# In-projection of a hybrid trunk: the gates' chunks first, then scan steps and token tiles in turn

## The chip, the core and the metric

The kernel runs on one core of a Trainium2 chip. The metric is the device time in microseconds, the median of several executions. The engines are named as in the profile: PE (TensorE, with PEld for its weight loads), DVE (VectorE), ACT (ScalarE), POOL (GpSimd) and SP (the queue that issues the DMAs). All arithmetic is float32; products are formed from a high and a low part in the fp32r form, three matmuls for each product (`mm3`).

## The reference

Two layers run over 9 tiles of 128 tokens: one tile of context and eight of a latent grid, 1024 features each. A layer multiplies its modulated input by `w_in` and cuts the result into parts:

```python
z = jnp.einsum('bsd,dn->bsn', h, P['w_in'][l])
hq, hff, hfb, hi, hg, mq, mkv, mkr, gq, gk, gv = jnp.split(z, IN_OFFSETS, axis=-1)
```

- hq, hff, hfb, hi and hg feed a gated linear scan (HGRN2), forward and backward, with 4 heads of 64: the two gates are sigmoids of hff and hfb, whose logarithms are summed along the tokens; the scan's query is silu(hq), its value hi; hg gates the scan's output.
- gq, gk and gv are query, key and value of a grouped attention (6 heads, 2 key heads), with an RMS norm of each head and a rotary embedding in two dimensions.
- mq, mkv and mkr feed a latent attention (6 heads).

What scan and attentions give is multiplied by `w_out`, added, normalised, and followed by a SwiGLU mixer. The modulation (`w_ada`) scales and shifts both halves of a layer.

## The kernel before

A layer has phases: `phase_b` (in-projection, scan), `phase_c` (attention), `phase_d` (out-projection), `phase_e` (mixer). The change lies in `phase_b` and `hgrn`.

**Chunks.** `w_in` is stored as eight chunks of 256 columns and one, "b", of 288. Chunk 0 is hq (the scan's query), 1 and 2 are the forward and backward gates, 4 is hi (the scan's value), 3 is hg, 5 is the first half of gq, 6 the rest of gq with gk, "b" is mkv, gv and mkr, 7 is mq. `w_in()` loads a chunk's weights and splits them into a high part (ACT, L103) and a low part (DVE or, for one chunk number, POOL, L104); they lie in a ring of 8 tiles, of which a chunk takes 4 (b: 6).

**Token chunks.** `token_chunk` takes one chunk through the 9 token tiles: 24 matmuls (8 row blocks, three products each, L110 to L112) into one bank, then an evacuation that depends on the chunk. Chunks 1 and 2: two sigmoids on ACT (L379, L380). Chunks 4 and 3: a copy on ACT (L373) and a store. Chunks 5 and 6: square and copy on ACT, a row sum on DVE (L412), an inverse root on POOL (L118, L119), two or three multiplies on DVE (L415, L417), the rotary embedding on POOL (L397 to L401), a store. Chunk b: a smaller form of that (L442 to L452). Chunk 7: L432 to L435. After every other token tile `self.fill()` puts in a half-step of the next modulation (L176), in layer 0 only, 16 half-steps in all. Chunk 0 is computed the other way round: its weights are the stationary operand, and each of six passes streams 384 tokens (L466 stores them by scan tile).

**Gates and scan.** `gates` takes the logarithms, in 9 steps, of both gates (L564 to L570: two Ln on ACT, four operations on DVE each); an ordering edge puts the Ln behind the last sigmoid of chunk 2. `hgrn` then walks over the 9 tiles. For each, `prep` forms the cumulative sums on PE and copies them (L598), loads value and query (L616, L618); `levels` runs 8 levels, -1 to 6: from level 0 on three subtractions on DVE (L641, L644), an Exp on ACT, two products on POOL (L648 for X, L650 for Q), four small matmuls on PE (L655) and two predicated copies on DVE (L660); `out` does the tile's output (L682) and the state's update. `prep` of the next tile is written between levels 2 and 3. X, Q and E have two buffers each.

**What sets the order.** The program is written as one stream. A planner gives each engine its own order: by its own estimate of times it takes, among the instructions whose inputs and buffers are free, the one written first. On the chip each engine follows that order and waits where an input is late. In the text the order is: chunk 0, chunk 1, constants, chunk 2, gates, chunk 4, the whole scan, chunks 3, 5, 6, b, 7 (with the GQA turns, L526 to L542, in chunk 7's evacuation), the gate of the scan's output (`hgrn_gate`, L720 to L729). Accumulators: layer 0 has two banks for chunks, layer 1 three.

Of the kernel before, what the change touches and what calls it, by code (L numbers as in the profile page):

```python
# [16 lines left out]
P = 128  # L17
# [16 lines left out]
TX = 3  # L34

# [18 lines left out]
class Build:  # L54
# [272 lines left out]
    def w_in(self, l, c):  # L327
# [4 lines left out]
        return [(k0, k0 + 4) + self.wsplit(A["w_in_a"][l, c, :, k0:k0 + 4, :], [4, 256], self.nc.gpsimd if c == 0 else None)  # L332
                for k0 in (0, 4)]

    def phase_b(self, l, first=None):
# [18 lines left out]

        def token_chunk(name, evac):
            ws = self.w_in(*name)
            n = 288 if name[1] == "b" else 256
            for t in range(NT):
                ps = self.ps("A")
                terms = [(self.hts(t, k, 0), self.hts(t, k, 1), hi[:, k - k0, :], lo[:, k - k0, :])  # L360
                         for k0, k1, hi, lo in ws for k in range(k0, k1)]
                self.mm3(ps[:, :n], terms)
                evac(t, ps)
                if t % 2:
                    self.fill()

        def stage():
            return self.t("b2", [P, 384], tag="st", bufs=3)
# [85 lines left out]

        ws = first or self.w_in(l, 0)
        for ci in range(3):
            for j in range(2):
                ps = self.ps("A")
                terms = [(hi[:, k - k0, j * P:(j + 1) * P], lo[:, k - k0, j * P:(j + 1) * P],
                          self.HT[ci][:, k, 0, :], self.HT[ci][:, k, 1, :])  # L460
                         for k0, k1, hi, lo in ws for k in range(k0, k1)]
                self.mm3(ps[:, :384], terms)
                sg = stage()
                nc.scalar.activation(sg[:, :384], ps[:, :384], AF.Sigmoid)
                nc.vector.scalar_tensor_tensor(sg[:, :384], ps[:, :384], 64 ** -0.5, sg[:, :384], op0=ALU.mult, op1=ALU.mult)
                nc.sync.dma_start(z["h"][3 * ci:3 * ci + 3, :, j, :].rearrange("t p s -> p t s"),  # L466
                                  sg[:, :384].rearrange("p (t s) -> p t s", t=3))

        token_chunk((l, 1), ev_f(0))
# [959 lines left out]
```

## Time and profile before

| | |
|---|---|
| median of 3 runs | 3788.2 us (3786.13 to 3790.14) |
| the profiled execution | 3788.79 us, span 3787.0 us |
| PE busy | 3667.2 us (97%) |
| DVE busy | 2021.7 us (53%) |
| ACT busy | 1380.3 us (36%) |
| POOL busy | 1100.7 us (29%) |
| mean granted PE clock | 0.981 |

The busy time of PE is a sum over the whole span, and a matmul counts as busy while it waits in PE's pipeline. The granted clock says in which part of a stretch PE ran at the upper of its two levels (1.00 is 2.4 GHz, 0.50 is 1.2 GHz). `phase_b` of layer 0 lies between about 36 and 490 us of the span, that of layer 1 between about 1955 and 2345 us.

### The profile page before, as it was taken

What the parts mean: (1) busy time and instruction counts of PE and PEld (TensorE: products, weight loads), DVE (VectorE), ACT (ScalarE), POOL (GpSimd) and SP (SyncE); (2) the same over time, 40 slices, a digit from 0 to 9 for tenths busy, and PEclk for the clock granted to TensorE, in tenths of its full rate; (3) what the DMA queues carried; (4) which work ended last, traced back from release to release, by engine and by line L of the source; (5) the groups of instructions that cost most, each with busy time, mean ns of one, the idle gap of its engine ahead of it and who ended that gap; (6) DMA issues with size and microseconds to landing.
All of it is one profiled execution on the core that took longest, in us unless ns stands there. A gap on an engine that the chain in (4) does not pass through costs nothing.

```text
span 3787.0 us, 60397 instructions
## 1 busy us (share of the span) xinstructions
PE 3667.2 (97%) x23734; PEld 3210.9 (85%) x23734; DVE 2021.7 (53%) x3906; ACT 1380.3 (36%) x3283; POOL 1100.7 (29%) x1394
## 2 busy tenths in 40 slices
PE   8999899999999999999999989999999999999997
PEld 6878777788788888999989878778877999999996
DVE  3489456556564333333366894665567533333336
ACT  3433466666341111111144335666654211111111
POOL 1158850211161000000432786511126600000054
PEclk9998899999999999999999998999999999999998
DMA  6521421001134331111231115100012311111131
GB/s 240 179 64 43 117 65 25 15 7 35 59 130 157 101 106 51 51 40 48 96 128 59 51 44 140 28 20 15 7 55 73 114 41 47 41 40 45 45 95 73
DMA packets 185967, 263.78 MB, mean 70 GB/s; under 512 B 68657, under 2 KB 114353, under 8 KB 185170
## 3 DMA queue, kind: packets, MB, share of 16 engines
q1 hardware_dynamic: 185682, 259.92, 21.7%
q8 instruction: 187, 3.06, 0.3%
q14 instruction: 98, 0.80, 0.1%
HBM read 218.47 MB, written 38.77 MB: 68 GB/s over the span
## 4 chain that ended last, share of the span: by engine, by line
PE 81%; DVE 7%; POOL 4%; ACT 3%; issue 2%; DMA 2%; SPq 0%; POOLq 0%; DVEq 0%; ACTq 0%
PE b L110 10%; PE b L112 10%; PE b L111 10%; PE d L855 7%; PE c L806 5%; PE a L110 5%; PE b L784 5%; PE a L111 4%; PE a L112 4%; PE a L784 3%; PE b L655 2%; PE c L110 2%; PE c L112 2%; PE c L111 2%; PE d L111 2%
## 5 line engine op out<-in xcount | busy, mean ns | idle before, releaser
L111 PE MATMUL b<-h,w 128*128 128x384 f32 x1848 | 622.4, 337 | 3.6 <-DVE h L104 2.7
L110 PE MATMUL b<-h,w 128*128 128x384 f32 x1848 | 623.8, 338 | 0.1
L112 PE MATMUL b<-h,w 128*128 128x384 f32 x1848 | 621.8, 337 | 0.0
L103 ACT CAST w<-raw 128x1024 fp32r<-128x1024 f32 (+2 forms) x192 | 198.7, 1036 | 803.4 <-PE c L111 262.7
L104 DVE TENSOR_TENSOR w<-raw,w 128x1024 fp32r<-128x1024 f32 (+3 forms) x188 | 242.1, 1295 | 367.9 <-ACT w L103 362.4
L110 PEld LDWEIGHTS b<-h,w 128*128 128x128 f32 x1848 | 347.4, 188 | 17.8 <-issue 7.6
L111 PEld LDWEIGHTS b<-h,w 128*128 128x128 f32 x1848 | 347.6, 188 | 10.3 <-DVE h L104 4.5
L112 PEld LDWEIGHTS b<-h,w 128*128 128x128 f32 x1848 | 347.5, 188 | 8.0 <-issue 5.0
L1245 POOL TENSOR_TENSOR acc<-acc,lg 128x512 f32<-128x512 f32 x36 | 49.1, 1378 | 935.4 <-DVE acc L1231 931.7
L110 PE MATMUL a<-w,h 128*128 128x256 f32 (+1 forms) x960 | 287.2, 299 | 8.4 <-DVE st L445 4.9
L855 PE MATMUL d<-pt,v 128*64 128x128 f32 x3456 | 288.9, 285 | 0.4 <-DVE m L856 0.4
L111 PE MATMUL a<-w,h 128*128 128x256 f32 (+1 forms) x960 | 281.0, 293 | 0.0
L112 PE MATMUL a<-w,h 128*128 128x256 f32 (+1 forms) x960 | 279.7, 292 | 0.0
L806 PE MATMUL c<-ident,p 128*128 128x128 f32 x1728 | 272.0, 279 | 6.7 <-ACT p L790 2.9
L855 PEld LDWEIGHTS d<-pt,v 128*64 128x64 f32 x3456 | 186.3, 136 | 76.7 <-issue 61.7
L785 DVE TENSOR_REDUCE m<-b 128x1 f32<-128x384 f32 x346 | 188.5, 554 | 112.8 <-PE b L784 112.1
L806 PEld LDWEIGHTS c<-ident,p 128*128 128x128 f32 x1728 | 200.4, 141 | 47.2 <-issue 16.3
L790 ACT ACTIVATE p<-b,nm 128x384 f32<-128x384 f32 x346 | 198.6, 582 | 72.4 <-DVE nm L788 66.3
L110 PEld LDWEIGHTS a<-w,h 128*128 128x128 f32 x960 | 188.1, 196 | 30.9 <-ACT m L380 6.7
L111 PEld LDWEIGHTS a<-w,h 128*128 128x128 f32 x960 | 188.1, 196 | 5.4 <-issue 1.9
L112 PEld LDWEIGHTS a<-w,h 128*128 128x128 f32 x960 | 187.5, 195 | 4.2 <-issue 1.7
L1202 DVE TENSOR_TENSOR gate<-gate,b 128x384 f32<-128x384 f32 x110 | 60.9, 553 | 242.5 <-PE b L112 242.5
(391 smaller groups left out, 8483.1 us busy)
## 6 DMA issues: line engine op xcount, KB each, us to landing
w<-in_w_ada_dram SPq DMA_DIRECT2D x96, 512.0 KB, 4.4
raw<-in_w_ffn_in_dram SPq DMA_DIRECT2D x88, 512.0 KB, 3.5
raw<-in_w_ffn_out_dram SPq DMA_DIRECT2D x44, 512.0 KB, 3.6
raw<-in_w_in_a_dram SPq DMA_DIRECT2D x32, 512.0 KB, 4.4
xs<-acc SPq DMA_DIRECT2D x36, 256.0 KB, 4.1
u<-xs SPq DMA_DIRECT2D x36, 256.0 KB, 2.5
raw<-in_w_out_dram SPq DMA_DIRECT2D x16, 512.0 KB, 4.3
tx<-zq SPq DMA_DIRECT2D x72, 96.0 KB, 2.4
```

The lines of the kernel that those rows point to most:

```text
L103: self.nc.scalar.copy(hi, src)
L104: (eng or self.nc.vector).tensor_tensor(lo, src, hi.bitcast(F32), op=ALU.subtract)
L110: self.nc.tensor.matmul(out, ah, bh, start=i == 0, stop=False)
L111: self.nc.tensor.matmul(out, ah, bl, start=False, stop=False)
L112: self.nc.tensor.matmul(out, al, bh, start=False, stop=i == n - 1)
L655: nc.tensor.matmul(ps[:, j * P:(j + 1) * P], X[r, j, :], Q[r, j, :], start=True, stop=True)
L784: nc.tensor.matmul(ps, a, bfn(c * 384, 384), start=k == 0, stop=k == len(ops) - 1)
L785: nc.vector.reduce_max(mx[:, c:c + 1], ps, axis=AX.X)
L790: nc.scalar.activation(pt[:, c * 384:(c + 1) * 384], tiles[c], AF.Exp, bias=nm, accum_out=sm[:, u, c:c + 1])
L806: nc.tensor.transpose(pt[:, (2 * i + u) * P:(2 * i + u + 1) * P], g["p"][u][:, kt * P:(kt + 1) * P], self.ident)
L855: nc.tensor.matmul(po[h * 64:(h + 1) * 64, :P], g["v"](k, h), turned[s // 2][:, o:o + P], start=k == 0, stop=k == 8)
L1202: nc.vector.tensor_tensor(g, g, ps[:, :384], op=ALU.mult)
```

## The change

Three things change in `phase_b`, one in `hgrn`.

- The order of the first chunks becomes 1, 2, gates, 0; the chunk whose low part POOL splits becomes number 1.
- `token_chunk` becomes a generator, `tiles`, that yields after every token tile, runs through several chunks, and asks for the next chunk's weights at token tile 4 of the present one.
- Chunks 4, 3, 5, 6 and b are one such generator. `hgrn` becomes a generator too, which yields after every level and after `out`, nine times for each scan tile; in five of the nine places a token tile is written. Chunk b so moves ahead of the end of the scan's pool; chunk 7 stays where it was.
- The load of the scan's value moves from `prep` to the head of `out`.

```diff
+TILE_TURNS = (0, 2, 4, 6, 7)
...
-        return [(k0, k0 + 4) + self.wsplit(A["w_in_a"][l, c, :, k0:k0 + 4, :], [4, 256], self.nc.gpsimd if c == 0 else None)
+        return [(k0, k0 + 4) + self.wsplit(A["w_in_a"][l, c, :, k0:k0 + 4, :], [4, 256], self.nc.gpsimd if c == 1 else None)
...
+        def tiles(*chunks, ws=None):
+
+            ws = ws or self.w_in(l, chunks[0][0])
+            for i, (name, evac) in enumerate(chunks):
+                n = 288 if name == "b" else 256
+                for t in range(NT):
+                    ps = self.ps("A")
+                    terms = [(self.hts(t, k, 0), self.hts(t, k, 1), hi[:, k - k0, :], lo[:, k - k0, :])
+                             for k0, k1, hi, lo in ws for k in range(k0, k1)]
+                    self.mm3(ps[:, :n], terms)
+                    evac(t, ps)
+                    if t % 2:
+                        self.fill()
+                    if t == 4 and i + 1 < len(chunks):
+                        nxt = self.w_in(l, chunks[i + 1][0])
+                    if t == NT - 1 and i + 1 < len(chunks):
+                        ws = nxt
+                    yield
+
         def token_chunk(name, evac):
...
+            for _ in tiles((name[1], evac)):
+                pass
...
-        ws = first or self.w_in(l, 0)
-        for ci in range(3):
...
-        token_chunk((l, 1), ev_f(0))
+        for _ in tiles((1, ev_f(0)), ws=first):
+            pass
...
         token_chunk((l, 2), ev_f(1))
         self.gates(l)
-        token_chunk((l, 4), ev_raw("i"))
-
-        self.hgrn(l, cst, masks)
-
-        token_chunk((l, 3), ev_raw("g"))
-        token_chunk((l, 5), ev_q(0))
-        token_chunk((l, 6), ev_q(1))
+
+        ws = self.w_in(l, 0)
+        for ci in range(3):
...
+        proj = tiles((4, ev_raw("i")), (3, ev_raw("g")), (5, ev_q(0)), (6, ev_q(1)), ("b", ev_k))
+        for n, _ in enumerate(self.hgrn(l, cst, masks)):
+            if n % 9 in TILE_TURNS:
+                next(proj)
+        for _ in proj:
+            pass
...
-        token_chunk((l, "b"), ev_k)
         token_chunk((l, 7), ev_mq)
...
-            it = self.t("b2", [P, 256], tag="it", bufs=2)
-            nc.sync.dma_start(it, z["i"][t])
...
         def out(t, ops):
...
+            bc, kT, q, at = ops
+            it = self.t("b2", [P, 256], tag="it", bufs=2)
+            nc.sync.dma_start(it, z["i"][t])
...
-            levels(t, ops, -1, 3)
+            yield from levels(t, ops, -1, 3)
             nxt = block(t + 1) if t + 1 < NT else None
-            levels(t, ops, 3, 7)
+            yield from levels(t, ops, 3, 7)
             out(t, ops)
+            yield
             ops = nxt
...
-        first = self.w_in(0, 0)
+        first = self.w_in(0, 1)
```

## Rows read from the trace of the kernel before

**Rows 1.** windows: start:end, length, busy us (x count) of PE, PEld, DVE, ACT, POOL, PEclk, DMA, GB/s

```profile
179.00:240.00 61.00, 61.00 (x431) 47.73 (x429) 46.25 (x110) 23.80 (x49) 27.50 (x33) 1.00 0.26 80
240.00:412.00 172.00, 158.31 (x1109) 138.68 (x1108) 156.92 (x360) 67.40 (x151) 146.65 (x193) 0.90 0.16 48
412.00:490.00 78.00, 65.58 (x463) 62.95 (x463) 17.80 (x40) 30.68 (x90) 49.97 (x109) 0.89 0.51 139
2060.00:2150.00 90.00, 89.18 (x695) 78.46 (x694) 76.65 (x179) 37.89 (x85) 62.11 (x81) 1.00 0.15 44
2150.00:2305.00 155.00, 142.34 (x965) 125.44 (x966) 126.75 (x303) 60.08 (x140) 131.83 (x200) 0.89 0.18 56
2305.00:2345.00 40.00, 35.38 (x286) 33.89 (x284) 12.18 (x22) 22.58 (x62) 32.48 (x58) 0.97 0.74 200
2345.00:2360.00 15.00, 11.03 (x58) 8.95 (x59) 8.14 (x21) 7.45 (x24) 3.21 (x5) 0.63 0.39 105
```

**Rows 2.** waits of TensorE from 240 to 412 us (total us, times, longest)

```profile
PE b L655 <- POOL Q L650: 7.0, 5, 2.1
```

**Rows 3.** timeline: scan's copies and last matmuls, chunk 7's last evacuation (start us, us, operation)

```profile
209.84 1.07 ACT L598 COPY bc<-c 128x512 f32<-128x512 f32 x2 [2.59 <-PE c L597]
...
374.18 0.57 ACT L598 COPY bc<-c 128x512 f32<-128x512 f32 x1
...
410.58 1.21 PE L655 MATMUL b<-Q,X 64*128 64x128 f32 x8 [1.54 <-POOL Q L650]
...
489.64 0.38 ACT L432 ACTIVATE t<-a 128x256 f32<-128x256 f32 x1 [0.69 <-PE a L112]
...
2090.96 0.59 ACT L598 COPY bc<-c 128x512 f32<-128x512 f32 x1 [2.70 <-PE c L597]
...
2143.26 0.59 ACT L598 COPY bc<-c 128x512 f32<-128x512 f32 x1 [0.68 <-PE c L597]
...
2304.88 0.56 PE L682 MATMUL c<-it,at 128*128 128x64 f32 x4
...
2339.67 0.37 ACT L432 ACTIVATE t<-d 128x256 f32<-128x256 f32 x1
```

**Rows 4.** timeline of ScalarE, layer 1: two token tiles of chunk 1

```profile
1977.46 0.38 ACT L380 ACTIVATE m<-a 128x256 f32<-128x256 f32 x1
...
1980.26 0.38 ACT L380 ACTIVATE m<-a 128x256 f32<-128x256 f32 x1
```

**Rows 5.** timeline of ScalarE: last sigmoid of chunk 2, first scan copy, both layers

```profile
138.84 0.38 ACT L380 ACTIVATE m<-a 128x256 f32<-128x256 f32 x1
...
170.81 1.07 ACT L598 COPY bc<-c 128x512 f32<-128x512 f32 x2
...
2025.89 0.38 ACT L380 ACTIVATE m<-d 128x256 f32<-128x256 f32 x1
...
2055.48 1.05 ACT L598 COPY bc<-c 128x512 f32<-128x512 f32 x2
```

**Rows 6.** groups of TensorE, 76 to 139 us (count, busy us, mean ns): modulation

```profile
L176 PE MATMUL d<-w,csr 128*32 128x512 f32 x64 | 10.6, 605 | 0.0
```

**Rows 7.** timeline of ScalarE at 171 us: a table load

```profile
171.91 1.28 ACT L667 ACT_TABLE_LOAD   x1
173.20 0.42 ACT L667 ACTIVATE m<-bc 128x256 f32<-128x256 f32 x1
```

**Rows 8.** DMA issues of the page (KB each, us to landing)

```profile
tx<-zq SPq DMA_DIRECT2D x72, 96.0 KB, 2.4
```

**Rows 9.** 240 to 412 us: instructions that touch tile st

```profile
240.00:412.00 172.00, 27.23 (x45) 7.56 (x21) 39.94 (x60) 0.90 0.16 48
```

**Rows 10.** groups of GpSimd from 240 to 412 us: L119

```profile
L119 POOL TENSOR_TENSOR r<-rsv,mhalf 128x4 f32<-128x4 f32 x18 | 19.8, 1104 | 0.3
```

**Rows 11.** groups of VectorE: L644 from 36 to 180 us, then 240 to 412

```profile
L644 DVE TENSOR_TENSOR E<-bc 128x128 f32<-128x128 f32 x6 | 1.6, 288 | 1.7 <-ACT bc L598 1.7
...
L644 DVE TENSOR_TENSOR E<-bc 128x128 f32<-128x128 f32 x86 | 36.6, 461 | 0.0
```

More of the change, by code (lines that the diff above doesn't have):

```diff
@@ L353, in phase_b @@
         self.z = z
-        def token_chunk(name, evac):
[L356 to L365, printed above, removed]
+        def tiles(*chunks, ws=None):
[15 more added lines that the diff above has]
+                    yield
+        def token_chunk(name, evac):
+            for _ in tiles((name[1], evac)):
+                pass
         def stage():
@@ L452, in ev_k @@
             nc.sync.dma_start(z["k"][t], st[:, :288])
-        ws = first or self.w_in(l, 0)
-        for ci in range(3):
[L457 to L467, printed above, removed]
-        token_chunk((l, 1), ev_f(0))
+        for _ in tiles((1, ev_f(0)), ws=first):
+            pass
         cst = {}
@@ L485, in phase_b @@
         self.gates(l)
-        token_chunk((l, 4), ev_raw("i"))
-        self.hgrn(l, cst, masks)
-        token_chunk((l, 3), ev_raw("g"))
-        token_chunk((l, 5), ev_q(0))
-        token_chunk((l, 6), ev_q(1))
+        ws = self.w_in(l, 0)
+        for ci in range(3):
+            for j in range(2):
+                ps = self.ps("A")
+                terms = [(hi[:, k - k0, j * P:(j + 1) * P], lo[:, k - k0, j * P:(j + 1) * P],
+                          self.HT[ci][:, k, 0, :], self.HT[ci][:, k, 1, :])
+                         for k0, k1, hi, lo in ws for k in range(k0, k1)]
+                self.mm3(ps[:, :384], terms)
+                sg = stage()
+                nc.scalar.activation(sg[:, :384], ps[:, :384], AF.Sigmoid)
+                nc.vector.scalar_tensor_tensor(sg[:, :384], ps[:, :384], 64 ** -0.5, sg[:, :384], op0=ALU.mult, op1=ALU.mult)
+                nc.sync.dma_start(z["h"][3 * ci:3 * ci + 3, :, j, :].rearrange("t p s -> p t s"),
+                                  sg[:, :384].rearrange("p (t s) -> p t s", t=3))
+        proj = tiles((4, ev_raw("i")), (3, ev_raw("g")), (5, ev_q(0)), (6, ev_q(1)), ("b", ev_k))
[4 more added lines that the diff above has]
+            pass
         self.close("b")
@@ L614, in prep @@
             nc.scalar.copy(kT.rearrange("p d j s -> p (d j s)"), ps)
-            it = self.t("b2", [P, 256], tag="it", bufs=2)
-            nc.sync.dma_start(it, z["i"][t])
             q = self.t(b, [P, 2, P], tag="qT", bufs=2)
             nc.sync.dma_start(q, z["h"][t])
-            return bc, kT, it, q
+            return bc, kT, q
         def strided(x, off, *dims):
@@ L624, in levels @@
         def levels(t, ops, lev0, lev1):
-            bc, kT, it, q, at = ops
+            bc, kT, q, at = ops
             av = at.rearrange("p (j e) s -> p e j s", e=2)
@@ L710, in hgrn @@
         for t in range(NT):
-            levels(t, ops, -1, 3)
+            yield from levels(t, ops, -1, 3)
             nxt = block(t + 1) if t + 1 < NT else None
-            levels(t, ops, 3, 7)
+            yield from levels(t, ops, 3, 7)
             out(t, ops)
+            yield
             ops = nxt
```

2 lines of the change are left out of this document (1 added, 1 removed).

## The prediction

> **What bounds the kernel now.** I read the page first (TensorE is busy for 97% of the span), then the stretches of the in-projection one by one, because an average of 97% hides where TensorE loses time. The reader should take two things from each stretch in [rows 1]: length minus TensorE busy (idle), and one minus the granted clock, times the length (time lost at the lower of the two levels, 1.2 instead of 2.4 GHz). Layer 0: 240 to 412 us loses 13.7 us idle and 0.10 x 172 = 17.2 us to the clock, 30.9 in all; 412 to 490 us loses 12.4 + 8.6 = 21.0. From 179 to 240 us TensorE loses nothing. Layer 1: 2060 to 2150 loses next to nothing (0.8 us); 2150 to 2305 loses 12.7 + 17.1 = 29.8, 2305 to 2345 4.6 + 1.2 = 5.8, 2345 to 2360 4.0 + 5.6 = 9.6. Together 97 us. The change adds and removes no matmul, so its gain comes out of these 97 us.
>
> Who causes the loss is in the same rows: from 240 to 412 VectorE is busy 156.92 of 172 us and GpSimd 146.65. That is the scan (self.hgrn) together with the query chunks, whose evacuation runs on both. TensorE executes in the order written down for it, so it stands at a scan matmul until GpSimd has made the operand [rows 2]. After the scan GpSimd stays busy, but what remains there for TensorE is chunk work that could have run earlier.
>
> The scan's pace is the spacing of its cumulative-sum copies at L598 [rows 3]: tiles 2 to 8 of layer 0 take (374.18 - 209.84)/6 = 27.4 us each; tiles 2 to 4 of layer 1, where TensorE is full, (2143.26 - 2090.96)/2 = 26.15. A token tile of a 256-wide chunk takes TensorE 2.80 us [rows 4], so five of them leave 26.15 - 14.0 = 12.15 us as the scan tile's own TensorE time.
>
> **The change, part by part.**
>
> *Chunk order.* Ahead of the scan stand today chunks 0, 1, 2 and 4; then 1, 2 and 0. One chunk is 9 x 2.80 = 25.2 us. Today layer 0 needs from the last sigmoid of chunk 2 at 138.84 to the first copy of the scan at 170.81 for the gates and chunk 4, layer 1 from 2025.89 to 2055.48 [rows 5]. The chain of the gates is unchanged and chunk 0 (144 matmuls 384 wide, the columns of a 256-wide chunk) covers it as chunk 4 did. So the scan starts 25.2 us earlier: layer 1 at 2030.3. In layer 0, four of the modulation's half-steps also slip behind the start; 8 of them are 64 matmuls in 10.6 us [rows 6], so 5.3 us: 140.3.
>
> *What stands under the logarithms.* Chunk 0 brings six Sigmoids among 18 Ln. ScalarE changes table for each change of function: one load takes 1.28 us and the next Exp starts 0.01 us after it [rows 7]. Bounds: 2 loads (as today) to 14, so 0 to 12 x 1.28 = 15.4 us of ScalarE per layer. I take 4 us, and nothing on the path, since token tiles of chunk 4 are ready as cover; without cover the scan starts up to 15.4 us later and the gain falls by as much per layer. The Trainium skill (ScalarE: Activation LUTs, What ACT_TABLE_LOAD costs) adds a drain of about 1.38 us to each switch; by it the upper end would be an estimated 32 us. Rows 7 do not show that drain, so I stay with the row.
>
> *Startup.* With two accumulator banks in layer 0, only two of the three token tiles of an HT block can collect while the block is built, where chunk 0 covered the whole block: 0 to 2.8 us lost, and modulation fills that may close holes. I take 0. The GpSimd split of the first chunk's low half moves along with the order, 0. The `it` load stands right before its use in the text, but its input is written tiles earlier and the planner may issue it when its buffer is free; 0, with one whole DMA wait for each of the 18 scan tiles as the other end: by a similar load from a scratch tensor [rows 8] 2.4 us each, 43 us.
>
> *The turns.* Five token tiles per scan tile: chunks 4 and 3 fill 18/5 = 3.6 scan tiles, the query chunks 5 and 6 another 3.6, chunk b 1.8.
> - Chunks 4 and 3 are evacuated by a ScalarE copy only: the TensorE-full pace, 3.6 x 26.15 = 94 us.
> - Query tiles cost VectorE 27.23/18 = 1.5 us and GpSimd (39.94 + 19.8)/18 = 3.3 us each at least [rows 9, 10]. Today 18 of them fall on 172/27.4 = 6.3 scan tiles, 2.9 per tile; then 5. The 2.1 more cost 3.2 us if VectorE sets the pace (30.6), 6.9 if GpSimd does (34.3). I take 32.5: 117 us.
> - Chunk b is 288 wide, 3.15 us a tile by width: 12.15 + 15.75 = 27.9 us, 50 us for 1.8 scan tiles.
>
> Sum 261 us, in layer 0 plus 5.3 for the displaced half-steps. The scan ends at 2030.3 + 261 = 2291 (today 2305 [rows 3]) and 140.3 + 266 = 407 (today 412).
>
> *After the scan.* I count the end of the in-projection as the window bounds 490 and 2345; the last evacuation of chunk 7 begins at 489.64 and 2339.67 [rows 3]. In layer 1 today 40 us follow on the scan, with the whole of chunk 7 and an end of chunk b. Then chunk 7 (25.2 us), the GQA turns and the gate of the scan's output remain, with GpSimd at 32.48 of 40 us [rows 1]; I take 36 us. Ends: 2327 against 2345, 18 us less; 443 against 490, 47 us less, because chunk b no longer stands there. Sum 65 us.
>
> *The same from the losses.* In this plan TensorE still loses 117 - 94 = 23 us per layer in the query part, 5.8 after each scan and 9.6 at the entry to attention in layer 1: 67 of the 97 us remain, which gives 30. The two sums disagree because today's busy time contains bubbles that the first does not carry over. I take the middle, 48 us.
>
> **Rivals.**
> - *Everything fits.* The planner spreads the query evacuations over the whole scan, and the query part runs at 26.15. That returns 23 us per layer: the first sum would be 111, over what is there, so I take some 85 of the 97: 3704. For it: 2060 to 2150 runs at a full clock with such a mix. Against it: GpSimd is at 85% from 240 to 412 already.
> - *VectorE and GpSimd exclude each other.* The scan's 128x128 subtraction takes 288 ns while GpSimd is nearly idle and 461 ns beside it [rows 11]. If their times add, the query part takes 27.4 + 2.1 x (1.5 + 3.3) = 37.5 us a tile, 5 x 3.6 = 18 us more per layer: gain 48 - 36 = 12, 3777. Against it: in today's 172 us the two are busy 303 us together, though the busy time contains blocking. The Trainium skill (SBUF — State Buffer, Who interferes with whom) states this as a rule: a VectorE instruction with two SBUF inputs and a GpSimd instruction that reads SBUF block each other entirely. The trace agrees in direction; how far is open.
> - *The turns hold the scan back* (slower). Today the scan is written first and the planner gives it every free slot; then a token tile stands ahead of the following scan step, in the in-order queues of GpSimd and VectorE too. TensorE's wait for GpSimd's Q is 7.0/5 = 1.4 us each time [rows 2]. If each of the 27 turns with a query or b tile holds a level back by that much, 27 x 1.4 x 2 = 76 us: 3741 + 76 = 3817. From 48/54 = 0.9 us per turn on there is no gain left. Against it: a level's operands have two buffers, so single delays are taken up.
> - *The change does nothing.* The planner already moves token tiles into the scan's gaps (query tiles run from the middle of the scan today), and until 240 and 2150 TensorE is full in any case, so the earlier start only moves the gaps: 3785.
>
> **How the numbers follow.** Profiled execution 3788.8 us (span 3787.0), median 3788.2, so no correction. Forecast 3788.8 - 48 = 3741, chance 0.48, own range 3719 to 3764. Everything fits 0.17, exclusion 0.20, nothing 0.06, held back 0.09. What a measurement here can tell from no change is 0.2%, 7.6 us: faster 0.48 + 0.17 + 0.20 = 0.85, same 0.06, slower 0.09. The range takes in the first rival nearly to its value and the second whole: 3703 to 3783; outside lie the slower case, half of "nothing" and the tip of the first rival.
>
> **What would show it.** Right: the first L598 copy some 25 us earlier in both layers; L442 (chunk b) before the last L655; the stretch from scan end to the last L432 at about 36 us in both layers; L598 spacing near 26 in the first tiles and 31 to 34 in the middle. Exclusion: a middle spacing of 37 with L644 over 461 ns. Held back: spacing over 31 in the first four tiles too, with TensorE waits for Q. Wrong altogether: scan start unmoved, or the last L432 not earlier than 490 and 2340.

## The result: slower, 3809 us for a forecast of 3741

The changed kernel takes 3809.0 us (median of 4 runs, 3807.4 to 3812.2) beside 3787.2 us for the kernel before on the same chip: 1.0056 times its time, 95% interval 1.0043 to 1.0069. The profiled execution has a span of 3806.8 us against 3787.0.

The head of the page of the changed kernel, and then its windows (columns as in rows 1):

```profile
span 3806.8 us, 60433 instructions
PE 3654.9 (96%) x23734; PEld 3203.1 (84%) x23734; DVE 2015.4 (53%) x3906; ACT 1413.3 (37%) x3309; POOL 1097.2 (29%) x1394
```

```profile
108.00:147.00 39.00, 29.03 (x165) 28.76 (x164) 18.20 (x40) 37.02 (x49) 1.45 (x2) 0.87 0.20 64
147.00:280.00 133.00, 131.78 (x1006) 107.34 (x1006) 89.69 (x218) 48.87 (x100) 56.60 (x71) 1.00 0.38 120
280.00:421.00 141.00, 122.32 (x872) 108.81 (x870) 115.61 (x276) 53.01 (x118) 121.64 (x166) 0.88 0.16 50
421.00:491.00 70.00, 61.08 (x437) 59.03 (x437) 12.92 (x27) 27.85 (x88) 45.08 (x101) 0.93 0.52 147
2003.00:2051.00 48.00, 35.94 (x213) 34.86 (x211) 33.76 (x55) 33.83 (x47) 5.88 (x2) 0.89 0.26 80
2051.00:2150.00 99.00, 98.58 (x786) 88.19 (x787) 80.06 (x183) 45.38 (x94) 53.90 (x64) 0.98 0.18 53
2150.00:2327.00 177.00, 156.99 (x1127) 142.24 (x1126) 132.67 (x301) 63.95 (x153) 145.99 (x225) 0.89 0.19 57
2327.00:2362.00 35.00, 31.31 (x250) 30.70 (x249) 9.46 (x19) 18.42 (x52) 26.76 (x48) 0.95 0.76 203
```

Read them as the prediction read [rows 1], idle time plus (1 - clock) x length. The first half of the scan loses next to nothing (147 to 280, 2051 to 2150). Its second half loses 18.7 + 16.9 = 35.6 us in layer 0 and 20.0 + 19.5 = 39.5 in layer 1, more than the 30.9 and 29.8 of before. And there are two new holes that before did not have, under the logarithms: 108 to 147 loses 10.0 + 5.1 and 2003 to 2051 loses 12.1 + 5.3. ScalarE is busy for 37.02 of 39 us in the first of them.

The scan itself, answering to [rows 3]: the copies that end a scan tile (L698), and the last evacuations of chunk 7 (L444). Timeline of ScalarE, changed kernel:

```profile
180.31 0.37 ACT L698 COPY m<-c 128x256 f32<-128x256 f32 x1 [0.98 <-PE c L696]
...
273.40 0.37 ACT L698 COPY m<-c 128x256 f32<-128x256 f32 x1 [0.51 <-PE c L696]
...
393.01 0.37 ACT L698 COPY m<-c 128x256 f32<-128x256 f32 x1 [3.26 <-PE c L696]
421.18 0.38 ACT L698 COPY m<-c 128x256 f32<-128x256 f32 x1
490.94 0.39 ACT L444 ACTIVATE t<-a 128x256 f32<-128x256 f32 x1 [0.64 <-PE a L113]
2079.48 0.37 ACT L698 COPY m<-c 128x256 f32<-128x256 f32 x1 [1.34 <-PE c L696]
2154.20 0.36 ACT L698 COPY m<-c 128x256 f32<-128x256 f32 x1
2281.01 0.37 ACT L698 COPY m<-c 128x256 f32<-128x256 f32 x1 [0.16 <-PE c L696]
2326.56 0.40 ACT L698 COPY m<-c 128x256 f32<-128x256 f32 x1
...
2361.95 0.39 ACT L444 ACTIVATE t<-d 128x256 f32<-128x256 f32 x1
```

The copies shown are the ends of scan tiles 0, 3, 7 and 8 of each layer. In layer 1 they give 24.9 us a tile in the raw part (beside chunks 4 and 3) and 31.7 in the query part (beside 5 and 6), both near the forecast's 26.15 and 32.5. But the last tile takes 45.6. In layer 0 the raw part takes 31.0 a tile and the query part 29.9. In layer 0 chunk 7 ends at 491, as before; in layer 1 it ends 22 us later than before. Two places explain this.

**Under the logarithms.** Timeline of ScalarE, changed kernel, layer 0. L494 is chunk 0's Sigmoid, L580 and L581 are the gates' Ln, L681 and L657 Exps of the scan:

```profile
117.82 0.62 ACT L580 ACTIVATE u<-u 128x512 f32<-128x512 f32 x1
118.45 1.28 ACT L494 ACT_TABLE_LOAD   x1
119.75 0.49 ACT L494 ACTIVATE st<-a 128x384 f32<-128x384 f32 x1
120.26 1.28 ACT L581 ACT_TABLE_LOAD   x1
121.55 0.63 ACT L581 ACTIVATE m<-m 128x512 f32<-128x512 f32 x1
...
124.21 1.28 ACT L681 ACT_TABLE_LOAD   x1
...
126.04 1.28 ACT L580 ACT_TABLE_LOAD   x1
127.33 0.63 ACT L580 ACTIVATE u<-u 128x512 f32<-128x512 f32 x1
127.98 1.28 ACT L657 ACT_TABLE_LOAD   x1
129.27 0.63 ACT L657 ACTIVATE E<-E 128x512 f32<-128x512 f32 x1
```

Three functions stand in turn where before there was one. Sixteen loads between 107 and 151 us take 20.5 us, against two (2.6 us) around the same logarithms before [rows 7 is the second of them]; layer 1 has 14. TensorE stands behind this. Its waits from 108 to 150 us, the end of that wait in its timeline, and then its waits from 280 to 421 (answering to [rows 2]):

```profile
PE a L111 <- DVE st L495: 10.0, 1, 10.0
...
136.23 0.69 PE L111 MATMUL a<-h,w 128*128 128x384 f32 x1 [9.97 <-DVE st L495]
...
PE b L666 <- POOL Q L661: 9.7, 7, 2.8
```

The first row is one wait of 10.0 us. L495 is the product right behind the Sigmoid, and until it has read the third pass of chunk 0 out of its accumulator bank, the fifth has no free one: the matmul that waits is 384 wide, so it is chunk 0's own. That third Sigmoid starts at 135.09, with seven of the loads between it and the second one at 119.75. Chunk 4's first matmul comes behind the sixth pass, at 146.94.

**The end of the scan.** Chunk b's evacuations (L454, first and last start), changed kernel, layer 0:

```profile
L454 ACT ACTIVATE t<-a x9: 259/278/283, 419.0 to 454.0; 128x128 f32<-128x128 f32 x9
```

Its turns are written into the last two scan tiles, yet its first tile is evacuated at 419.0, two us before the scan ends. The query tiles were late by then, and 70 us of chunk work follow the scan instead of 36. In layer 1 all nine tiles of b stand in the last scan tile (evacuated from 2294.0 to 2326.1). The four scan tiles before it hold 15 token tiles, all of them query tiles, where the turns write 20. Their copies on ScalarE, from 2154.5 to 2281.2 us:

```profile
L421 ACT COPY st<-a x10: 362/366/383, 2165.2 to 2276.0; 128x256 f32<-128x256 f32 x10
L421 ACT COPY st<-d x5: 363/366/385, 2160.5 to 2257.9; 128x256 f32<-128x256 f32 x5
```

### The profile page after: what moved, and what is told of

It reads as the page before. It is cut to its first block, busy times and chain, and to the rows that moved or that the text cites. A ratio compares the mean times of both kernels' runs of the same rounds, so it can differ in the third digit from the quotient of the medians.

```text
span 3806.8 us, 60433 instructions
## 1 busy us (share of the span) xinstructions
PE 3654.9 (96%) x23734; PEld 3203.1 (84%) x23734; DVE 2015.4 (53%) x3906; ACT 1413.3 (37%) x3309; POOL 1097.2 (29%) x1394
## 5 line engine op out<-in xcount | busy, mean ns | idle before, releaser
L805 ACT ACTIVATE p<-b,nm 128x384 f32<-128x384 f32 x346 | 198.5, 581 | 70.7 <-DVE nm L803 61.8
L111 PEld LDWEIGHTS a<-w,h 128*128 128x128 f32 x960 | 191.1, 199 | 28.2 <-issue 6.1
L112 PEld LDWEIGHTS a<-w,h 128*128 128x128 f32 x960 | 191.1, 199 | 7.0 <-issue 2.5
L113 PEld LDWEIGHTS a<-w,h 128*128 128x128 f32 x960 | 190.4, 199 | 7.7 <-issue 5.1
```

The lines of the kernel that those rows point to most:

```text
L111: self.nc.tensor.matmul(out, ah, bh, start=i == 0, stop=False)
L112: self.nc.tensor.matmul(out, ah, bl, start=False, stop=False)
L113: self.nc.tensor.matmul(out, al, bh, start=False, stop=i == n - 1)
L805: nc.scalar.activation(pt[:, c * 384:(c + 1) * 384], tiles[c], AF.Exp, bias=nm, accum_out=sm[:, u, c:c + 1])
```

## Experiments

Every kernel was timed beside the kernel before. Medians of 4 to 11 executions, and ratios to the kernel before with their 95% intervals. The kernel before itself had medians from 3787.2 to 3789.3, so a difference of 2 us between two rows says nothing:

```
changed kernel                                    3809.0  1.0056 [1.0043, 1.0069]
1  changed, no Sigmoid in chunk 0                 3793.7  1.0018 [1.0009, 1.0027]
2  chunk order only                               3815.0  1.0072 [1.0059, 1.0084]
3  turns only                                     3802.8  1.0045 [1.0033, 1.0058]
4  turns only, chunk 4 whole ahead of the scan    3786.5  0.9996 [0.9987, 1.0005]
5  as 1, scan's Exps behind the last Ln           3784.6  0.9989 [0.9980, 0.9997]
6  as 3, scan's Exps behind the last Ln           3795.2  1.0017 [1.0008, 1.0025]
7  changed, chunk b behind the scan               3814.2  1.0067 [1.0055, 1.0080]
8  as 4, output gate by Exp                       3782.0  0.9984 [0.9975, 0.9993]
9  as 5, query tiles copied only                  3708.8  0.9783 [0.9769, 0.9796]
10 changed, chunk b's norm on GpSimd              3812.8  1.0059 [1.0046, 1.0072]
11 as 8, with 10's edit                           3781.6  0.9980 [0.9971, 0.9989]
12 before, output gate by Exp                     3792.5  1.0011 [1.0002, 1.0020]
13 as 6, turns spread, no fills in them           3762.0  0.9925 [0.9912, 0.9938]
14 as 13, output gate by Exp                      3754.6  0.9907 [0.9893, 0.9921]
15 as 8, half spread                              3769.0  0.9948 [0.9934, 0.9963]
16 changed, turns spread, no fills in them        3776.6  0.9967 [0.9956, 0.9979]
17 as 6, no fills in the turns                    3780.6  0.9975 [0.9967, 0.9984]
18 order of changed, no loads in turn, spread     3753.6  0.9905 [0.9890, 0.9921]
```

Two causes were to be weighed: function loads under the logarithms, and the query tiles' work on VectorE and GpSimd. Where an expectation gives a theory a letter, it says there what it stands for. Unless a run says otherwise it computes the whole reference.

**1, 5: the loads.** Run 1 takes the Sigmoid of chunk 0 away (the scan's query is left without its silu); run 5 also issues the scan's Exps behind the last Ln.

```diff
-                nc.scalar.activation(sg[:, :384], ps[:, :384], AF.Sigmoid)
+                nc.scalar.copy(sg[:, :384], ps[:, :384])
...
+        def exp(*a):
+            with self.tc.issue_after(self.last_ln.ins):
+                return nc.scalar.activation(*a, AF.Exp)
```

> The changed kernel, but chunk 0 is evacuated by a plain copy where the Sigmoid stood, so its scan query is not silu (the two ScalarE instructions take the same time); nothing else differs. Theory A (table loads): from the end of chunk 2 to the start of the scan ScalarE alternates between Ln and Sigmoid, 13 loads of 1.28 us per layer where the kernel before has 2; TensorE's accumulators stay full behind them, and the two stretches lose 10 + 5 us (layer 0, 108 to 147) and 12 + 5 us (layer 1, 2003 to 2051). Without the Sigmoid these 32 us come back: 3809 - 32 = 3777, between 3770 and 3784, 2 table loads per layer before the scan, TensorE idle below 2 us in both stretches. Theory B (the turns): the loads only move idle time that the slower scan would give back anyway; the time stays within 8 us of 3809.

> The changed kernel without any alternation of tables at the gates: chunk 0 is evacuated by a plain copy (its scan query is not silu), as in the run without the Sigmoid, and every Exp of the scan is ordered behind the last Ln. The run without the Sigmoid (3794) still had 5 to 7 loads per layer there, from the scan's first Exp among the later tiles' Ln, and lost 4.0 + 1.4 us (layer 0, 108 to 180) and 4.3 + 3.7 us (layer 1, 1998 to 2060). Theory A (all table loads at the gates): that 13 us comes back, 3781 (3776 to 3787), no loads between the first Ln and the last, TensorE idle under 2 us in both windows. Theory B (the turns): still 3790 or more, since the loss is in the scan's last tile (layer 1: 66 us from the last kT copy to the scan's end where the kernel before has 46).

Run 1 gave back 15 us; its expectation missed because seven loads remain in layer 0 and five in layer 1, of the scan's Exp among the Ln. Run 5 gave 24.4 us, to 3784.6 (3781 was expected). Its scan tiles end as follows (timeline of ScalarE, run 5, L702 is the L698 of above):

```profile
167.08 0.37 ACT L702 COPY m<-c 128x256 f32<-128x256 f32 x1 [0.98 <-PE c L700]
...
2055.82 0.37 ACT L702 COPY m<-c 128x256 f32<-128x256 f32 x1 [0.87 <-PE c L700]
2131.13 0.35 ACT L702 COPY m<-c 128x256 f32<-128x256 f32 x1
2257.91 0.37 ACT L702 COPY m<-c 128x256 f32<-128x256 f32 x1 [0.15 <-PE c L700]
2302.59 0.40 ACT L702 COPY m<-c 128x256 f32<-128x256 f32 x1
```

In layer 1 the ends are 23.1 to 24.0 us earlier than the changed kernel's, with nearly the same spacing: the loads shift the scan and do little else. Some 9 us of this come over from layer 0 (chunk 1's first Sigmoid of layer 1 starts at 1947.45 in place of 1956.85). The loads account for 24 us. But the whole now only equals the kernel before: the rest of the forecast's gain is lost elsewhere.

**2, 3, 4, 6: order and turns apart.** Run 2 is the kernel before with chunks 1, 2, 0, 4 ahead of the scan and no turns; run 3 keeps the order 0, 1, 2 and has the turns; run 6 is run 3 with run 5's second edit; run 4 is run 3 with

```diff
-        proj = tiles((4, ev_raw("i")), (3, ev_raw("g")), (5, ev_q(0)), (6, ev_q(1)), ("b", ev_k))
+        token_chunk((l, 4), ev_raw("i"))
+        proj = tiles((3, ev_raw("g")), (5, ev_q(0)), (6, ev_q(1)), ("b", ev_k))
```

and four turns a scan tile.

> The kernel before with the new order of the first chunks alone (1, 2, gates, 0, then 4 and the whole scan, no turns). Theory A: the alternating table loads are here too, so it is slower than before by what the stretch loses, less what an earlier start of the scan returns: chunk 4 still stands ahead of the scan, so nothing starts earlier, and 15 to 32 us are lost: 3802 to 3819. Theory B: the order is harmless, 3780 to 3790.

> The changed kernel with the old order of the first chunks (0, 1, 2, gates), so that only the turns are left: chunks 4, 3, 5, 6 and b one token tile at a time between the scan's levels. No Sigmoid stands among the Ln. Theory A: 3765 to 3785, faster than before by a little or a lot, since the turns do no harm; two table loads per layer before the scan. Theory B: the turns hold the scan back, 3795 to 3815, with L609/L611 spacing of 30 us or more per scan tile.

> As the kernel with the turns alone, but chunk 4 is whole ahead of the scan as in the kernel before, and the turns hold chunks 3, 5, 6 and b, four token tiles for each scan tile. Theory A: 3770 to 3790. Theory B: between the kernel before and the one with all turns, 3790 to 3805. If chunk 4 among the turns is what costs or gains, this run and the one with the turns alone differ by 10 us or more.

> The kernel with the turns alone (3803) and every Exp of the scan ordered behind the last Ln; it computes the whole reference. Theory A: the turns cost only because chunk 4 no longer keeps the scan's first Exp away from the gates' Ln (7 table loads per layer, 6.0 + 1.4 us lost in 138 to 210, 7.1 + 6.8 us in 2031 to 2093): 3803 - 19 = 3784 (3778 to 3790), like the kernel with turns after chunk 4 (3786). Theory B: 3795 or more; the rest is then in the scan's last tile.

The order alone costs 27 us over before, with 26 loads around its logarithms in the two layers (4 before). The turns alone cost 15; 7.6 of that are six loads a layer, between the Ln and the scan's Exp, which run 6 takes out. Where chunk 4 stands whole between gates and scan, as in before and in run 4, the Exps come after the last Ln by themselves. Each part loses alone, and the two don't add up (22 together), so one hides part of the other.

**9: the query tiles' evacuation taken away.** Run 5 with chunks 5 and 6 evacuated by one ScalarE copy; their norm and rope are left out.

```diff
+        def ev_qr(half):
+            def ev(t, ps):
+                st = stage()
+                nc.scalar.copy(st[:, :256], ps[:, :256])
...
-        proj = tiles((4, ev_raw("i")), (3, ev_raw("g")), (5, ev_q(0)), (6, ev_q(1)), ("b", ev_k))
+        proj = tiles((4, ev_raw("i")), (3, ev_raw("g")), (5, ev_qr(0)), (6, ev_qr(1)), ("b", ev_k))
```

> The run without alternation (3785) with the query chunks 5 and 6 evacuated by one ScalarE copy: no norm, no rotary embedding, which takes some 18 x 1.5 us of VectorE and 18 x 3.3 us of GpSimd out of each scan stretch; queries and keys of the GQA, and the scan query, are not the reference's. In that run the scan starts 41 us (layer 0) and 36 us (layer 1) earlier than before, but its stretch is 276 and 278 us long where it was 236 and 245, and TensorE still loses 36 us in each (idle 19 to 22, clock 14 to 17). Theory C (VectorE and GpSimd are full there): without the query evacuations the losses fall from 36 to under 10 us per layer and the time by 45 to 60: 3725 to 3740. Theory D (TensorE's own work sets the length, and its losses are waits in a fixed order for GpSimd's Q and the predicated copies, whatever else runs there): 5 to 25 us less, 3760 to 3780, with scan tiles of 26 us or more throughout.

75.8 us less than run 5. The windows of its two scans:

```profile
135.00:397.00 262.00, 261.91 (x2049) 225.06 (x2048) 178.79 (x435) 97.21 (x220) 124.95 (x181) 1.00 0.27 87
1985.00:2227.00 242.00, 239.39 (x1939) 216.57 (x1938) 176.83 (x436) 99.56 (x225) 128.44 (x187) 1.00 0.20 62
```

TensorE is full (0.1 and 2.6 us idle) at a granted clock of 1.00, where run 5 loses some 38 us a layer (135 to 411 and 2025 to 2303). So what the scan loses, it loses to the query tiles' evacuation, and the scan steps and turns by themselves hold nothing back. Most of that work is on VectorE and GpSimd; a square on ScalarE and its temporary tile go with it, and which of them holds TensorE back this run does not tell.

**7, 10: chunk b.** Run 7 puts chunk b behind the scan again with four turns a tile. Run 10 moves the product of b's norm to GpSimd, because VectorE waits 24.0 us for GpSimd's root at that line (L457) from 2260 to 2330 us.

```diff
-        proj = tiles((4, ev_raw("i")), (3, ev_raw("g")), (5, ev_q(0)), (6, ev_q(1)), ("b", ev_k))
+        proj = tiles((4, ev_raw("i")), (3, ev_raw("g")), (5, ev_q(0)), (6, ev_q(1)))
...
-            nc.vector.scalar_tensor_tensor(st[:, :128], ps[:, :128], r, rows[:, 384:512], op0=ALU.mult, op1=ALU.mult)
+            nc.gpsimd.tensor_scalar(st[:, :128], st[:, :128], r, None, op0=ALU.mult)
+            nc.gpsimd.tensor_tensor(st[:, :128], st[:, :128], rows[:, 384:512], op=ALU.mult)
```

> The changed kernel with chunk b back behind the scan, four turns per scan tile for chunks 4, 3, 5 and 6. Theory B in its narrow form (chunk b in the scan's last tile: VectorE stands 24 us in 7 waits of L457 for GpSimd's root, with the scan's subtractions queued behind it): the last tile of layer 1 falls from 67 us to about 46, but chunk b then stands after it as in layer 0 of the kernel before: 3800 (3790 to 3808). If chunk b in the turns is a gain: 3812 to 3830. The table loads at the gates stay, 13 per layer.

> The changed kernel with chunk b's norm multiplied on GpSimd (two more instructions there per token tile, from a ScalarE copy of the whole row) instead of on VectorE from PSUM; it computes the whole reference. VectorE then never stands behind GpSimd's root in chunk b. Theory (L457 holds the scan's last tile): from the last kT copy to the scan's end in layer 1 67 us becomes 48 to 55, the time 3809 - 12 = 3797 (3790 to 3803). Rival: the last tile is long because TensorE has nine tiles of chunk b in it (9 x 3.15 us): unchanged, 3805 to 3812.

Neither gains (3814.2 and 3812.8). In run 10 the last scan tile of layer 1 falls from 45.6 to 33.1 us, but three tiles of b then follow the scan. So VectorE's wait at L457 is a symptom, and the length of the last tile is the work in it: by the prediction's prices one scan tile, one query tile and nine of b are 12.15 + 2.80 + 9 x 3.15 = 43.3 us of TensorE.

**8, 11, 12: the output gate.** In run 4 chunk 7 ends some 13 us earlier than before in layer 1 (2326.9 against 2339.7), yet the time is the same. Behind it the gate's Sigmoid (L740) then stands among the attention's Exps (L805). Loads of run 4 from 2290 to 2355 us (groups of ScalarE), and its window at the attention's entry, which loses 12.8 us in 21, where before lost 9.6 in 15 [rows 1]:

```profile
L740 ACT ACT_TABLE_LOAD x4 | 5.1, 1283 | 0.1
L805 ACT ACT_TABLE_LOAD x4 | 5.1, 1283 | 0.1
```

```profile
2334.00:2355.00 21.00, 13.68 (x72) 10.06 (x72) 7.47 (x18) 19.34 (x41) 7.62 (x12) 0.74 0.34 96
```

```diff
-                nc.scalar.activation(sg, g, AF.Sigmoid)
+                nc.scalar.activation(sg, g, AF.Exp, scale=-1.0)
+            nc.vector.tensor_scalar(sg, sg, 1.0, None, op0=ALU.add)
+            nc.vector.reciprocal(sg, sg)
```

> The kernel with turns after chunk 4 (3786), with the scan's output gate (hgrn_gate) formed by Exp, an addition and a reciprocal on VectorE instead of a Sigmoid; it computes the whole reference. That kernel ends chunk 7 11 us earlier than the one before in layer 0 and 13 us earlier in layer 1, but loads tables 6 times from 412 to 433 us and 6 times from 2334 to 2352 us, where the gate's Sigmoid meets the Exp of the scan and of the attention. Theory A, carried to the end of the scan: without these loads 8 to 14 us come back, 3774 (3770 to 3780), faster than the kernel before. If the tables cost nothing there: 3786.

> The fastest so far (turns after chunk 4, output gate by Exp, 3782) with chunk b's norm multiplied on GpSimd as well; the whole reference. There the last scan tile of layer 0 takes 62 us from its kT copy, with chunk b in it. If VectorE's waits for the root set that: 3770 (3764 to 3777). If TensorE's own work does: 3779 to 3784.

> The kernel before with nothing changed but the output gate by Exp; the whole reference. It has 3 table loads of the gate in layer 0 and 5 in layer 1 that go: 3 to 8 us less if each costs TensorE its 1.28 us (3780 to 3785), nothing if they stand beside other work. If it comes out at 3782 the turns after chunk 4 bring nothing at all, and all of that run's 6 us are the tables'.

The edit gives 4.5 us on run 4 (8 to 14 were expected) and 7.4 on run 13 (run 14 below), and costs 4 on the kernel before, where the gate's loads stand apart from the attention. Single differences of this size are near what these runs can tell apart, and where the rest of run 4's 13 us went is not settled. Run 10's edit on top of it (run 11) changes nothing.

**13, 14, 15, 17: the turns spread.** Run 13 lets raw and query tiles take turns, so that a scan tile is given 2.5 of each in place of 5 of one. It also leaves the modulation's filling matmuls out of these turns (they run later); run 17 does that alone, in the old order.

```diff
+        def pair(a, b):
+            return mixed(tiles(a, fills=False), tiles(b, fills=False), 1)
+
-        proj = tiles((4, ev_raw("i")), (3, ev_raw("g")), (5, ev_q(0)), (6, ev_q(1)), ("b", ev_k))
+        proj = chain(pair((4, ev_raw("i")), (5, ev_q(0))), pair((3, ev_raw("g")), (6, ev_q(1))), tiles(("b", ev_k)))
```

> The kernel of the sixth run (old chunk order 0, 1, 2, scan's exponentials issued behind the last logarithm, five turns per scan tile) with the turns' order changed: tiles of chunks 4 and 5 in turn, then of 3 and 6 in turn, then of b; the filling matmuls in the raw tiles of these pairs are left out. Nothing of the computation changes. Each scan tile of the first seven then meets 2.5 query tiles and 2.5 raw tiles in place of five of one kind. Theory C, spread (the scan stretch loses TensorE time because five query tiles beside a scan tile ask more of VectorE and GpSimd than TensorE's own time there; evenly spread they ask about 25 us of VectorE and 21 us of GpSimd in a tile where TensorE needs 26 to 31 us): the scan stretch's TensorE loss falls from some 35 us a layer to 15 or less, 3755 us (3735 to 3775). Rival D, fixed order (each engine's written order makes TensorE wait for a query tile's evacuation wherever it stands, or the weights of two chunks at a time stand late): the loss stays, 3790 us (3780 to 3805).

> The run above, with the output gate's sigmoid behind the scan written as an exponential, plus one, and reciprocal (the exponential's function loads stay away from the attention's). Nothing of the computation changes. If the loads of the gate's sigmoid among the next stage's exponentials cost time on TensorE's path, 4 to 10 us less than the run above; if they only fill ScalarE's idle time, the same within 3 us.

> The kernel of the eighth run (old chunk order, chunk 4 whole ahead of the scan, turns of 3, 5, 6 and b, four per scan tile, gate by the exponential) with chunks 3 and 5 in turn, then 6, then b; no filling matmuls in the pair. Nothing of the computation changes. Theory C, spread: queries then stand beside scan tiles 0 to 4 at two a tile and beside 5 to 7 at four: about half of the loss of the query part goes, 3768 us (3755 to 3778). Rival D: as the eighth run, 3782 us (3778 to 3795).

> The kernel of the sixth run with the filling matmuls left out of the tiles of chunks 4, 3, 5 and 6, in their old order: the control for the spread turns, which leave them out too. Nothing of the computation changes; the same filling work is done later. If spreading was the cause of the gain, this stays near the sixth run, 3795 us (3788 to 3802). If leaving the fillings out was, it comes near the spread run, 3762 us (3755 to 3772).

Windows of the two scans in run 6, in run 17 and in run 13, in this order:

```profile
153.00:416.00 263.00, 244.50 (x1781) 208.33 (x1779) 212.93 (x492) 102.42 (x217) 179.08 (x236) 0.93 0.23 74
2050.00:2319.00 269.00, 245.51 (x1822) 218.47 (x1821) 221.26 (x504) 112.29 (x251) 202.22 (x295) 0.94 0.19 59
```

```profile
152.00:422.00 270.00, 245.49 (x1840) 216.75 (x1838) 216.18 (x496) 106.11 (x237) 197.93 (x277) 0.94 0.21 64
2039.00:2299.00 260.00, 239.86 (x1786) 213.99 (x1785) 223.14 (x503) 104.47 (x241) 196.26 (x286) 0.95 0.18 57
```

```profile
152.00:414.00 262.00, 254.46 (x1925) 221.68 (x1924) 215.30 (x497) 102.07 (x238) 194.45 (x283) 0.98 0.23 71
2030.00:2284.00 254.00, 241.44 (x1850) 213.99 (x1849) 215.19 (x493) 107.09 (x248) 198.54 (x285) 0.99 0.21 63
```

VectorE and GpSimd are about as busy in all three (213 to 223 and 179 to 203 us a scan). The scans lose 76 us in run 6, 74 in run 17 and 28 in run 13: spreading is what fills TensorE, and its clock comes back with it, from 0.93 to 0.98 and 0.99. By its evacuations run 13 has done 5 and 8 query tiles when the first scan tile ends (layers 0 and 1) and meets mostly 2 a tile behind it, so part of the gain could be an earlier start of the queries; in run 16 below, with 2 or 3 from the first tile to the seventh, the same edit gives as much. The time falls from run 6 by 14.6 us without the fills and by 18.6 more with the spread, 33.2 in all. (The 18.6 are less than the 46 us that the scans lose less: other stretches lose more in run 13, from 2299 to 2400 us 13.7 us idle against 10.7, and these losses are a rough ledger, as said below.) Run 15, with half of the spread, stands between run 8 and run 14 as expected (3769.0). The control's expectation missed: it gave almost half of the gain, though not in the scan. Groups of TensorE, modulation matmuls, run 6 from 140 to 280 us, then run 17 from 280 to 421 and from 421 to 470:

```profile
L177 PE MATMUL d<-w,csr 128*32 128x512 f32 x64 | 11.6, 605 | 0.0
```

```profile
L177 PE MATMUL d<-w,csr 128*32 128x512 f32 x16 | 3.2, 605 | 0.0
...
L177 PE MATMUL d<-w,csr 128*32 128x512 f32 x32 | 5.5, 619 | 3.4 <-DMA w<-in_w_ada_dram 3.4
```

In run 6 these 11.6 us stand beside raw tiles, where TensorE is full; left for later, they stand where it has holes. By size that is 11.6 of the 14.6 us; the other 3 are not traced.

**16, 18: back to the changed kernel.** Run 16 is the changed kernel with run 13's spread alone. Run 18 has the changed order and everything above: chunk 0 evacuated by a copy, its silu taken in the scan's preparation, behind the last Ln, the spread, and the gate by Exp.

```diff
             nc.sync.dma_start(q, z["h"][t])
+            eq = self.t(b, [P, 2, P], tag="eq", bufs=2)
+            with self.tc.issue_after(self.last_ln.ins):
+                nc.scalar.activation(eq, q, AF.Exp, scale=-1.0)
+            nc.gpsimd.tensor_scalar(eq, eq, 1.0, None, op0=ALU.add)
+            nc.vector.reciprocal(eq, eq)
+            nc.vector.scalar_tensor_tensor(q, q, 64 ** -0.5, eq, op0=ALU.mult, op1=ALU.mult)
```

> The changed kernel with one edit: the turns go to tiles of chunks 4 and 5 by turns, then of 3 and 6, then of b, without the filling matmuls in these pairs. Nothing of the computation changes; the order 1, 2, 0 and the function loads among the logarithms stay. If the bunching of the query tiles and the function loads are two separate losses, the 33 us that the same edit gave on the sixth run come here too: 3776 us (3766 to 3788). If the earlier scan start had hidden one under the other (the loads' stall only shifts work that would wait later anyway), the edit gives less than 20 us: 3790 us or more.

> The changed kernel's order 1, 2, 0 with all that the runs point to: chunk 0 evacuated by a copy, its silu taken in the scan's own preparation by an exponential, plus one (GpSimd), reciprocal and product (VectorE), behind the last logarithm; the scan's exponentials behind it too; turns spread in pairs; the output gate by the exponential. The whole computation is done. Expected: the spread run with the gate by the exponential less the 10 us that lay between the fifth and the sixth run, 3745 us (3738 to 3755). Rival: the silu's three operations a scan tile on VectorE and GpSimd give the losses back, 3755 to 3765 us.

Run 16 is 32.4 us faster than the changed kernel, as forecast from run 13: the two causes are separate. It still has the hole under the logarithms (29.83 us of TensorE in the 39 from 108 to 147). Chunk b's evacuations in run 16:

```profile
L454 ACT ACTIVATE t<-a x9: 260/278/292, 361.5 to 415.9; 128x128 f32<-128x128 f32 x9
```

Now they lie inside the scan, which ends at 418, and chunk 7 ends 36 us later, at 454. Run 18 and run 14 compute the whole reference, beat the kernel before by 0.9% and the changed one by 1.4%, and can't be told apart (3753.6 and 3754.6). So once TensorE is full, the scan's earlier start is worth nothing that these runs show; run 18 pays for it with three more operations a scan tile on VectorE and GpSimd.

## Why the prediction was wrong, step by step

- *What bounds the kernel* held. What the scan loses comes from the query tiles' evacuation (run 9), and it shows as TensorE's idle time plus clock. As a ledger it is rough: TensorE is busy 12.3 us less on the page of after than on that of before with the same 23734 matmuls, so a difference of losses overstates the difference in time by about that much.
- *Chunk order, 25.2 us earlier* (30.5 in layer 0, with the half-steps) held once the loads are gone, with some over in layer 0: the first scan tile ends at 167.1 and 2055.8 in run 5. In before (timeline of ScalarE; L684 is the same copy):

```profile
205.69 0.37 ACT L684 COPY m<-c 128x256 f32<-128x256 f32 x1 [1.35 <-PE c L682]
...
2087.89 0.37 ACT L684 COPY m<-c 128x256 f32<-128x256 f32 x1 [0.98 <-PE c L682]
```

  That is 38.6 and 32.1 us, some 5 of the 32.1 because layer 1 itself begins earlier in run 5 (chunk 1's first Sigmoid at 1947.45; before at 1977.46, behind chunk 0's 25.2). In the changed kernel 25.4 and 8.4 were left. (Its first scan copy, my sign for this, stands at 122.61 and 2040.70, 48.2 and 14.8 us earlier than before; it runs among the logarithms there and says little of the scan.)
- *What stands under the logarithms* **failed**, first cause, 24 us (run 5). The bounds were 0 to 15.4 us of ScalarE a layer; I took 4, and nothing on the path, "since token tiles of chunk 4 are ready as cover". In fact there were 16 loads in layer 0, 14 more than before or 18 us, over my upper end, and 14 in layer 1, at it, because I counted only chunk 0's Sigmoids. The scan's own Exps come up among the Ln too, once no whole chunk keeps them apart. And the cover did not cover: chunk 4's tiles stand behind all six passes of chunk 0, need the same accumulator banks and the same ScalarE, and the fifth pass itself waited 10.0 us for a bank. The drain that the Trainium skill adds to a switch of tables (ScalarE: Activation LUTs, What ACT_TABLE_LOAD costs) shows in no row here either: the Sigmoid at 119.75 starts 0.02 us after its load's end at 119.73.
- *The turns*: **failed**, second cause. The paces in layer 1 look right (24.9 and 31.7 us a tile against 26.15 and 32.5), but by luck: a scan tile of the query part held 3.75 token tiles there, not 5, so the four of b that did not fit went into the last tile (45.6 us, 18 more than I took). The term that was too small is the price of the query tiles. I took 117 - 94 = 23 us of loss a layer for them; the windows of the query part and what follows it in the scan (280 to 421, 2150 to 2327) lose 35.6 and 39.5. Run 9 shows that this loss goes with the query evacuation, runs 13 and 17 that it shrinks when the same queries stand evenly.
- *After the scan*, 36 us: 35 in layer 1, but 70 in layer 0, where "chunk b no longer stands there" was wrong by 34 us. With the spread (run 16) these 36 are found.
- *Where fills go* was costed only for the scan's start. Beside raw tiles they stand on the path (run 17, 14.6 us). In the changed kernel 48 of the modulation's matmuls (10.6 us) lie between 180 and 274 us, which is why layer 0's raw part takes 31.0 us a tile with TensorE full, 15 us more than three times 26.15; I had charged 5.3, for the four half-steps that slip.
- *The middle of two sums*, 48 us: the sum from losses (30) assumed that nothing new would be lost and the other was built on b in its turns. Neither held.

Of the rivals, *everything fits* needed an order that spreads the queries. I left that to the planner, which had no such order; written out, it takes the changed kernel to 3776.6 (run 16) and, without the loads and the gate's Sigmoid, to 3753.6 (run 18), not to the 3704 of that rival. *Exclusion* did not show its sign (a spacing of 37), but it is not refuted. With 3.75 query tiles in place of 5 its own sum gives 27.4 + 0.85 x 4.8 = 31.5 us a tile, beside the measured 31.7, and mine, (32.5 - 27.4)/2.1 = 2.4 us for each query tile over 2.9, gives 29.5; its loss of 23 + 18 = 41 us a layer is near the measured 35.6 and 39.5. So the price of a query tile was nearer to its VectorE and GpSimd times added than to mine. Whether the two hold each other up, or something else makes a query tile as dear, no run tells. The scan's subtraction, 461 ns on average in [rows 11], takes 434 in the same part of the changed kernel (groups of VectorE, 280 to 421 us, and the spread of the same 62: shortest, median, longest):

```profile
L655 DVE TENSOR_TENSOR E<-bc 128x128 f32<-128x128 f32 x62 | 24.7, 434 | 0.0
...
L655 DVE TENSOR_TENSOR E<-bc x62: 274/282/1354, 282.0 to 408.7; 128x128 f32<-128x128 f32 x62
```

The mean stands for no single instruction: half of them take no more than 282 ns, as beside an idle GpSimd (288 in [rows 11]), and single ones up to 1354.

*The turns hold the scan back* had the sign and, by chance, nearly the size (3817), but not the mechanism: with the query work gone the turns cost nothing (run 9), and TensorE's waits for Q from 280 to 421 are 9.7 us in 7.

Without the loads the change comes to 3784.6 (run 5), next to the rival *nothing* (3785) and not far from *exclusion* (3777). From 3809 the measured edits take 24.4 (loads), 32.4 (spread and fills) and 7.4 (gate by Exp), which would make 3744.8; run 18, which has all three, stands at 3753.6. The 9 us between are not settled; its added operations in the scan are the likeliest place.

Not tried: the changed kernel with more accumulator banks in layer 0, which would tell how much of the 10.0 us wait is banks and how much is ScalarE. Nor a deeper ring of temporary tiles (`tmp`, two buffers). A query tile's square on ScalarE (L420) and its rotary embedding on GpSimd take theirs from the same ring, and from 2150 to 2327 us ScalarE waits 12.2 us in 6 for the embedding's last step (L413) before a square, in the queue in which the scan's Exps stand too. Run 9 takes this away with the rest, so how much of the query part's loss is engine time and how much these two buffers is open.

## What to carry over

Before moving work beside a stretch of ScalarE, list every function that becomes ready in that stretch, also of the work that now starts earlier, and count the alternations. Cover counts only if it uses neither the engine nor the buffers that are blocked. When two streams share TensorE, give each step of the one an even share of what the other asks of every engine: a mean that fits over the stage loses where it is bunched, and filling belongs where TensorE has holes.

## What the runs showed of the hardware

- Ln and Exp, each beside the other, loaded a table at each change (126.04 and 127.98 us in the timeline above, 1.28 us each). The Trainium skill (ScalarE: Activation LUTs, Table sets: the hidden batching unit) lists one set that holds both and needs a single load; in this program the loads were there, so the trace decides.
- The granted clock went with TensorE's holes in one and the same stage, the scan of layer 0: 0.93 on average with 18.5 us of idle time in run 6, 0.98 with 7.5 in run 13; 0.93 with 18.6 in run 5 (135 to 411 us) and 1.00 with 0.1 in run 9, where only the work of other engines had changed. In run 6 the clock doubles what the holes cost (18.5 us idle, 0.07 x 263 = 18.4 us of clock).
- VectorE and GpSimd were busy 215 and 194 us in a scan of 262 (run 13, layer 0), so at least 147 us at once, and TensorE still kept to 97%. The sum of their busy times is no bound of the scan's length; nor are they work alone, since the same subtraction above was busy for anything from 274 to 1354 ns.
